# A hybrid attention block: the gates' stage in written order, decays in steps between its products, branch units in other places

## The chip, the cores and the metric

The kernel runs as one program on one core of a Trainium2 chip. The metric is the device time of one execution in microseconds. Before the change it is 2083.89 us, the median of 3 runs (2081.26 to 2083.93). On the core, TensorE multiplies matrices, VectorE and ScalarE do elementwise work, GpSimd helps with small things, and SyncE (SP) issues most of the DMA transfers, in the order of its queue.

## The reference

One layer of a streaming encoder works on 1024 frames and 16 meta tokens of width 1024, batch 1, all in float32:

```python
h = h + 0.5 * swiglu(rmsnorm(h, ffn1_norm), ...)
u = rmsnorm(h, mix_norm)
(aq, ak, av, gq, gk, gv, gr, g_low, gate_a, gate_b) = jnp.split(u @ w_in, offsets, axis=-1)
ya = window_sink_attention(aq, ak, av, att_sinks)         # 8 heads, 2 key heads, chunks of 64
z = g_low @ gla_gate_w + gla_gate_b
log_a = jax.nn.log_sigmoid(z) / 16
og = gated_linear_attention(gq, gk, gv, log_a)            # 4 heads, a recurrence over chunks
yb = rmsnorm(og, gla_out_norm) * jax.nn.silu(gr)
mixed = sigmoid(gate_a) * (ya @ w_branch_att) + sigmoid(gate_b) * (yb @ w_branch_gla)
h = h + mixed @ w_out
h = h + 0.5 * swiglu(rmsnorm(h, ffn2_norm), ...)
return rmsnorm(h, final_norm)[:, N_META:]
```

The change touches the two gates (`gate_a`, `gate_b`, 1024 columns each), the decays made from `log_a`, and the product `ya @ w_branch_att`.

## The kernel before

Activations lie with their features on the 128 partitions and tokens along the free axis. A float32 matrix product is done as three products of halves: `split` or `halves` cast a value to a high half on ScalarE (line 235 for activations and weights of this stage, line 132 for 1024-wide weights) and subtract it on VectorE to get the low half (lines 236 and 133). One pass of one 128 x 128 weight tile over 512 tokens is one matmul on TensorE.

The stages of the middle of the program, in order: plain projections (`together`, lines 915 to 928), the low-rank projection of the decay gate (`low_rank`, lines 941 to 950), the gates' stage, projections and window attention (from line 1114), the linear attention (`Gla`, from line 1433), and the branch of the linear attention with its gate (`ev_b`, line 1551).

**The gates' stage** computes 16 column groups of 128, for the two gates, in 8 pairs. A pair is a 2 x 2 block product with seven instead of eight block products (`PRODUCTS`, line 154, with sums of weight blocks S1 to S4 and of activations T1 to T4). Each product is 12 matmuls (line 460). `gate_pair` loads two weight tiles with DMA, `Group.sums` makes S1 to S4 on VectorE (line 443), `Group.weights` makes the two halves of a product's weights, and copies and additions take the sums out of PSUM into blocks called x, which go to the `gates` buffer in DRAM. Sigmoid isn't applied here, but where a gate is used: in `ev_a` (line 1371) for the attention branch and in `ev_b` for the other. After the pairs 2 to 12, `decay` (line 1051) does one of six pieces: for each of two head pairs two halves of 512 frames and the 16 meta tokens. A piece has one small matmul into the tile z (line 1056), then Abs, Exp and Ln on ScalarE, running sums on VectorE (line 1064), four more Exp, and products with the queries and keys, which go to DRAM. In this program the engines' order in this stage is set by the framework's scheduler.

T4 takes the place of an activation tile half (lines 1000 to 1004), saved in `b12_dram`; it is loaded back at the end of the stage (line 1106). Weight tiles come from a ring (`ring_tile`): six of the pool `w_main` and two of `w_more`. Blocks x, s and those of the decays come from one pool of 17.

**The branch units.** `branch_units` (line 1349) gives four units for 256 columns of the attention branch: two column groups for the first 512 tokens (chunk 0) and two for the last 512. A unit is 12 matmuls, a load of the gate, and `ev_a`. There are 16 units in the list `fill`: two are done in the attention's last two slots, four ahead of the linear attention, the rest between its steps (line 1525), the last one behind them. `out_gate` (line 1502) finishes a head of the linear attention with transposes into the tile ot. The recurrence runs over 8 steps for each of two head pairs (`products`, `step`).

Of the kernel before, what the change touches and what calls it, by code (L numbers as in the profile page):

```python
# [14 lines left out]
ALU = mybir.AluOpType  # L15
# [20 lines left out]
def hybrid_kernel(  # L36
# [968 lines left out]

    def gate_pair(m):

        pair = []
        for i in range(2):
            pair.append(raw_tile())  # L1010
            c = C_GA + (m + i) * P
            nc.sync.dma_start(out=pair[-1].rearrange("p (k m) -> p k m", k=KT),
                              in_=w_in[:, c:c + P].rearrange("(k p) m -> p k m", p=P))
        g = Group(g8, *pair)
        cols = [k * P for k in range(4)]

        def product(i):
            return g.product(i, g.weights(i), g8.tops, cols, 0, m)

        def keep(i, c, x):  # L1020
            nc.sync.dma_start(out=gates[m + i, :, c * 512:(c + 1) * 512], in_=x)

        b = product(0)
        x11, x22 = g8.block("x11"), g8.block("x22")
        nc.scalar.copy(x11, b)
        a = product(1)
        nc.vector.tensor_add(x11, a, x11)
        g.sums(nc.vector)
        keep(0, 0, x11)
        product(2)  # L1030
        x12 = g8.block("x12")
        nc.scalar.copy(x12, b)
        d = product(3)
        nc.scalar.copy(x22, d)
        product(4)
        nc.vector.tensor_add(x22, b, x22)
        keep(1, 1, x22)
        product(5)
        nc.vector.tensor_add(x12, d, x12)
        keep(0, 1, x12)  # L1040
        product(6)
        x21 = g8.block("x21")
        nc.scalar.copy(x21, b)
        keep(1, 0, x21)

# [5 lines left out]
    def decay(p, c0, n):  # L1051
# [5 lines left out]
        nc.scalar.activation(e, ps, AF.Abs, bias=bg)  # L1057
        nc.vector.tensor_scalar(b, ps, bg, 0.0, op0=ALU.add, op1=ALU.min)

        nc.scalar.activation(e, e, AF.Exp, scale=-1.0)  # L1060
        nc.scalar.activation(e, e, AF.Ln, bias=1.0)
        w = min(n, P)
        for a in range(0, n, w):
            nc.vector.tensor_tensor_scan(b[:, a:a + w], b[:, a:a + w], e[:, a:a + w], 0.0, op0=ALU.add, op1=ALU.subtract)
        if n == NM:
            nc.vector.tensor_scalar(e, b, -1.0, b[:, n - 1:n], op0=ALU.mult, op1=ALU.add)
            nc.scalar.activation(e, e, AF.Exp, scale=1.0 / 16.0)
            nc.vector.tensor_mul(e, k, e)
            nc.sync.dma_start(out=km_dram[p], in_=e)
            return  # L1070
        q, d = g8.block("q"), g8.block("d")
        nc.sync.dma_start(out=q, in_=gq_dram[p, :, c0:c0 + n])
        by = lambda t: t.rearrange("p (a b) -> p a b", b=P)
        at = lambda i: by(b)[:, :, i:i + 1].to_broadcast([P, n // P, P])

        def out(x, src):
            nc.sync.dma_start(out=scaled_dram[x][p, :, c0:c0 + n], in_=src)


        nc.scalar.activation(e, b, AF.Exp, scale=1.0 / 16.0)  # L1080
        nc.vector.tensor_copy(dec[p][:, c0 // P:(c0 + n) // P, :], by(e)[:, :, P - 1:P])
        nc.vector.tensor_mul(e, q, e)
        out("qi", e)
        nc.vector.tensor_tensor(by(d), at(P - 1), by(b), op=ALU.subtract)
        nc.scalar.activation(d, d, AF.Exp, scale=1.0 / 16.0)
        nc.vector.tensor_mul(d, k, d)
        out("kd", d)
        e = g8.block("e")
        nc.vector.tensor_tensor(by(e), by(b), at(63), op=ALU.subtract)
        nc.scalar.activation(b, e, AF.Exp, scale=1.0 / 16.0)  # L1090
        nc.vector.tensor_mul(q, q, b)
        out("qm", q)
        nc.scalar.activation(e, e, AF.Exp, scale=-1.0 / 16.0)
        nc.vector.tensor_mul(k, k, e)
        out("km", k)

    pieces = [(p, c0, n) for p in range(2) for c0, n in CH_FR + [(S, NM)]]
    for m in range(0, 16, 2):
        if m == 14:
            g8.ring = [w_main] * 6  # L1100
        gate_pair(m)
        if 2 <= m <= 12:
            decay(*pieces.pop(0))
    for k in range(4):
# [265 lines left out]
    def ev_a(ps, m, c0, n, g):  # L1370
        nc.scalar.activation(g, g, AF.Sigmoid)
        nc.vector.tensor_mul(g, ps[:, 0:n], g)
        nc.sync.dma_start(out=gates[m, :, c0:c0 + n], in_=g)
# [3 lines left out]
    for m0 in range(0, KT, 2):  # L1377
        views = [(slice(g * 64, g * 64 + 64), lambda r: r.rearrange("p (k m) -> p k m", k=4),
                  w_branch_att[g * 256:(g + 1) * 256, m0 * P:(m0 + 2) * P].rearrange("(i d) m -> d i m", d=64)) for g in range(2)]
        fill += branch_units(views, ya, m0, load_a, ev_a)  # L1380

# [137 lines left out]
    for p in range(2):  # L1519
        g = heads[p]  # L1520
        g.begin()
        g.products(0)
        g.state()
        for j in range(8):
            if j % 4 != 3 and len(fill) > 1:
                fill.pop(0)()
            if p == 1 and j in (1, 3, 5, 7):
                out_gate(j // 4, CH_FR[(j // 2) % 2:(j // 2) % 2 + 1])
            if j < 7:
                g.products(j + 1)  # L1530
            g.step(j)
        g.end()
# [233 lines left out]
```

## Time and profile before

| | |
|---|---|
| median of 3 runs | 2083.89 us |
| the profiled execution | 2084.47 us |
| its span, first to last instruction | 2082.8 us |
| TensorE matmul busy | 2014.3 us, 97% |
| VectorE busy | 1401.3 us, 67% |
| ScalarE busy | 890.3 us, 43% |
| mean granted TensorE clock | 0.985 |

The shares are averages over stages. TensorE's matmuls are pipelined, so a busy TensorE can still run at the lower of its two clock levels; the granted clock is a column of its own. Idle time of an engine counts where TensorE waits for it. In a timeline, the number in brackets is how long the engine had stood idle before the row, and what it waited for.

### The profile page before, as it was taken

To read this page: it belongs to the slowest core of one execution; us is meant where nothing else is said; L and a number is where in the kernel's file an instruction comes from. 1 tells how busy PE (TensorE), PEld (TensorE's weight loads), DVE (VectorE), ACT (ScalarE), POOL (GpSimd) and SP (SyncE) were. 2 spreads that over 40 slices of the span, in tenths; PEclk is the share of its full clock that TensorE was granted. 3 is DMA by queue.
4 is the path that set the end of the run, shared out by engine and by line. 5 is a ranking of instruction groups with operands and counts; after the bars stand their busy time and mean duration, and the time that the engine had idled before them with its cause. 6 is when DMAs were issued, how large, how long until landed. Compare 5 with 4: busy or idle time off the path is not lost.

```text
span 2082.8 us, 32065 instructions
## 1 busy us (share of the span) xinstructions
PE 2014.3 (97%) x12084; PEld 1782.2 (86%) x12084; DVE 1401.3 (67%) x2441; ACT 890.3 (43%) x1727; POOL 177.9 (9%) x205
## 2 busy tenths in 40 slices
PE   8899999999999999788999999999999999999998
PEld 8899999999999987566889867888888888878888
DVE  5866676676778784544357647757876776767885
ACT  5534444443322353444356645434444444442222
POOL 1000000001222000000500000020000000013212
PEclk9999999999999999899999999999999999999999
DMA  6333354349985342433412364752453453599822
GB/s 202 106 113 123 128 177 146 118 160 362 348 288 171 106 130 76 131 122 112 116 49 62 116 217 136 246 170 81 133 192 130 142 182 122 174 373 360 289 96 82
DMA packets 285772, 343.06 MB, mean 165 GB/s; under 512 B 26406, under 2 KB 192032, under 8 KB 285616
## 3 DMA queue, kind: packets, MB, share of 16 engines
q1 hardware_dynamic: 267968, 279.60, 40.5%
q10 hardware_dynamic: 17296, 61.29, 7.8%
q8 instruction: 95, 1.56, 0.3%
q14 instruction: 61, 0.50, 0.1%
q0 software_dynamic: 352, 0.11, 0.1%
HBM read 220.66 MB, written 120.27 MB: 164 GB/s over the span
## 4 chain that ended last, share of the span: by engine, by line
PE 89%; DMA 3%; ACT 3%; DVE 3%; issue 1%; SPq 0%; DVEq 0%; ACTq 0%; POOLq 0%
PE pb L460 30%; PE pd L460 16%; PE pa L460 9%; PE z L460 3%; PE pj L103 2%; PE pj L104 2%; PE pj L105 2%; PE br L103 1%; PE wo L103 1%; PE wo L105 1%; PE wo L104 1%; PE br L104 1%; PE br L105 1%; DMA f1mid<-kh 1%; PE pd L841 1%
## 5 line engine op out<-in xcount | busy, mean ns | idle before, releaser
L460 PE MATMUL pb<-tt,wop 128*128 128x260 f32 (+1 forms) x2040 | 343.5, 322 | 0.0
L460 PEld LDWEIGHTS pb<-tt,wop 128*128 128x128 f32 x2040 | 299.3, 188 | 29.0
L235 ACT CAST wop<-s 128x512 fp32r<-128x512 f32 x264 | 162.1, 621 | 241.2 <-PE pb L460 95.7
L236 DVE TENSOR_TENSOR wop<-s,wop 128x512 fp32r<-128x512 f32 x264 | 184.7, 708 | 89.2 <-ACT wop L235 88.6
L460 PE MATMUL pb<-tm,wop 128*128 128x260 f32 (+1 forms) x1440 | 235.9, 320 | 5.8 <-DVE h L347 3.5
L460 PEld LDWEIGHTS pb<-tm,wop 128*128 128x128 f32 x1440 | 208.6, 190 | 25.5 <-DVE h L347 4.0
L235 ACT CAST wop<-raw 128x512 fp32r<-128x512 f32 x198 | 122.4, 623 | 235.3 <-PE pb L460 105.2
L236 DVE TENSOR_TENSOR wop<-raw,wop 128x512 fp32r<-128x512 f32 x198 | 139.5, 710 | 28.3 <-ACT wop L235 27.8
L443 POOL TENSOR_TENSOR s<-raw 128x512 f32<-128x512 f32 x28 | 37.1, 1324 | 1057.2 <-DMA tm<-f1mid 454.8
L460 PE MATMUL pd<-tt,wop 128*128 128x260 f32 (+1 forms) x708 | 121.2, 324 | 0.1
L347 DVE SCALAR_TENSOR_TENSOR h<-pb,h 128x520 f32<-128x520 f32 (+1 forms) x136 | 93.9, 693 | 39.7 <-PE pb L460 37.6
L460 PE MATMUL pd<-tm,wop 128*128 128x260 f32 (+1 forms) x720 | 118.8, 319 | 0.0
L460 PEld LDWEIGHTS pd<-tt,wop 128*128 128x128 f32 x708 | 104.6, 188 | 11.2 <-DVE wop L236 0.6
L460 PE MATMUL pb<-tb,wop 128*128 128x260 f32 (+1 forms) x672 | 112.3, 320 | 0.5 <-ACT vec L94 0.5
L460 PEld LDWEIGHTS pd<-tm,wop 128*128 128x128 f32 x720 | 104.3, 188 | 9.4
L460 PE MATMUL pd<-tb,wop 128*128 128x260 f32 (+1 forms) x672 | 112.2, 320 | 0.0
L460 PE MATMUL pa<-tb,wop 128*128 128x260 f32 (+1 forms) x672 | 112.0, 320 | 0.0
L460 PEld LDWEIGHTS pb<-tb,wop 128*128 128x128 f32 x672 | 97.9, 188 | 10.0 <-ACT vec L94 0.6
L460 PEld LDWEIGHTS pd<-tb,wop 128*128 128x128 f32 x672 | 97.8, 188 | 9.4
L460 PEld LDWEIGHTS pa<-tb,wop 128*128 128x128 f32 x672 | 97.8, 188 | 9.4
L443 DVE TENSOR_TENSOR s<-raw 128x512 f32<-128x512 f32 x94 | 64.6, 688 | 56.6 <-DMA raw<-in_ffn_w_up 54.9
L347 DVE SCALAR_TENSOR_TENSOR h<-pd,h 128x520 f32<-128x520 f32 (+3 forms) x112 | 72.6, 654 | 33.7 <-PE pd L460 17.5
(446 smaller groups left out, 4163.8 us busy)
## 6 DMA issues: line engine op xcount, KB each, us to landing
tm<-f1mid ACTq DMA_DIRECT2D x56, 520.0 KB, 6.4
tm<-f2mid ACTq DMA_DIRECT2D x56, 512.0 KB, 6.2
raw<-in_ffn_w_gate SPq DMA_DIRECT2D x42, 512.0 KB, 3.9
raw<-in_ffn_w_up SPq DMA_DIRECT2D x42, 512.0 KB, 4.1
raw<-in_ffn_w_down SPq DMA_DIRECT2D x80, 256.0 KB, 5.4
f1mid<-kh SPq DMA_DIRECT2D x70, 260.0 KB, 3.1
f1mid<-kl SPq DMA_DIRECT2D x70, 260.0 KB, 3.0
f2mid<-kh SPq DMA_DIRECT2D x70, 256.0 KB, 2.8
```

Source lines behind the costliest of these rows:

```text
L103: nc.tensor.matmul(ps, wh[k], xh[k], start=(k == 0), stop=False)
L104: nc.tensor.matmul(ps, wh[k], xl[k], start=False, stop=False)
L105: nc.tensor.matmul(ps, wl[k], xh[k], start=False, stop=(k == n - 1))
L235: nc.scalar.copy(x[:, 0:n], src)
L236: nc.vector.tensor_sub(x[:, n:2 * n], src, x[:, 0:n].bitcast(F32))
L347: nc.vector.scalar_tensor_tensor(hm, ps, 0.5, hm, op0=ALU.mult, op1=ALU.add)
L443: (eng.tensor_add if add else eng.tensor_sub)(a[s], a[x], a[y])
L460: nc.tensor.matmul(ps, y, z[:, s0:s0 + sn], start=(first and k == 0 and at == 0), stop=(at == 2 and k == len(cols) - 1), skip_group_check= ...
L841: nc.tensor.matmul(ps, y, x[:, c0 + s0:c0 + s0 + sn], start=(n == 0), stop=(n == 3 * LAST - 1), skip_group_check=True)
```

## The change

The gates' stage is written as one loop over pairs and products, and ScalarE, VectorE and TensorE take its instructions in the order in which the code is written (`manual_schedule`). The weights of a product are split two products ahead, over the pair's end too; the next pair's sums are made in the last step of a pair. The next pair's weight tiles are loaded a pair earlier, into two pools in turn, and the ring has only the six tiles of `w_main`. `decay` is now a generator: it stops at each `yield`, and one step of it follows each product. The decays lie in the last four pairs, with two pieces in the second and fourth of them. The eight column groups of the attention gate get Sigmoid in this stage, in place (line 1018 of the changed kernel), so `ev_a` has none. The units of the branch come in another sequence (the first four all for chunk 0), fewer of them stand between the steps of the recurrence, and four stand behind it.

```diff
-    def gate_pair(m):
+    def gate_weights(m):
         pair = []
         for i in range(2):
-            pair.append(raw_tile())
+            pair.append(g8.ext_tile() if m % 4 else raw_tile())
...
+        return Group(g8, *pair)
+
+    def gate_out(m, i, c, x):
+        if m < KT:
+            nc.scalar.activation(x, x, AF.Sigmoid)
+        nc.sync.dma_start(out=gates[m + i, :, c * 512:(c + 1) * 512], in_=x)
+
+    def gate_evac(m, i, ps, xs):
+        if i in (0, 2, 3, 6):
+            x = xs[i] = g8.block("x")
+            nc.scalar.copy(x, ps)
+            if i == 6:
+                gate_out(m, 1, 0, x)
+        else:
+            x = xs[{1: 0, 4: 3, 5: 2}[i]]
+            nc.vector.tensor_add(x, ps, x)
+            gate_out(m, *{1: (0, 0), 4: (1, 1), 5: (0, 1)}[i], x)
...
         nc.scalar.activation(e, ps, AF.Abs, bias=bg)
         nc.vector.tensor_scalar(b, ps, bg, 0.0, op0=ALU.add, op1=ALU.min)
+        yield
         nc.scalar.activation(e, e, AF.Exp, scale=-1.0)
+        yield
         nc.scalar.activation(e, e, AF.Ln, bias=1.0)
+        yield
...
+        nc.vector.tensor_tensor(by(d), at(P - 1), by(b), op=ALU.subtract)
+        nc.vector.tensor_tensor(by(f), by(b), at(63), op=ALU.subtract)
+        yield
...
         nc.scalar.activation(e, b, AF.Exp, scale=1.0 / 16.0)
+        nc.scalar.activation(d, d, AF.Exp, scale=1.0 / 16.0)
         nc.vector.tensor_copy(dec[p][:, c0 // P:(c0 + n) // P, :], by(e)[:, :, P - 1:P])
+        yield
         nc.vector.tensor_mul(e, q, e)
         out("qi", e)
...
+    AHEAD, cols = 2, [k * P for k in range(4)]
+    g8.ring = [w_main] * 6
+    group, follow = gate_weights(0), gate_weights(2)
+    made = [group.weights(i) for i in range(AHEAD)]
+    group.sums(nc.vector)
+    manual = tc.manual_schedule(engines={nc.scalar.engine, nc.vector.engine, nc.tensor.engine})
+    manual.__enter__()
     for m in range(0, 16, 2):
-        if m == 14:
-            g8.ring = [w_main] * 6
-        gate_pair(m)
-        if 2 <= m <= 12:
-            decay(*pieces.pop(0))
+        others = [decay(*x) for x in pieces.pop(0)] if m >= KT else []
+        xs = {}
+        for i in range(7):
+            j = i + AHEAD
+            if j < 7:
+                made.append(group.weights(j))
+            elif follow:
+                made.append(follow.weights(j - 7))
+                if j == 8:
+                    follow.sums(nc.vector)
+            gate_evac(m, i, group.product(i, made.pop(0), g8.tops, cols, 0, m), xs)
+            for o in others:
+                next(o, None)
+        group, follow = follow, gate_weights(m + 4) if m + 4 < 16 else None
+    manual.__exit__(None, None, None)
...
     def ev_a(ps, m, c0, n, g):
-        nc.scalar.activation(g, g, AF.Sigmoid)
         nc.vector.tensor_mul(g, ps[:, 0:n], g)
...
-        fill += branch_units(views, ya, m0, load_a, ev_a)
+        fill.append(branch_units(views, ya, m0, load_a, ev_a))
+    fill = fill[0][0:2] + fill[1][0:2] + fill[0][2:4] + fill[1][2:4] + fill[2] + fill[3]
...
-            if j % 4 != 3 and len(fill) > 1:
+            if j % 2 == 0 and len(fill) > 4:
                 fill.pop(0)()
```

ScalarE before, from a pair's last copy (line 1043) over a decay piece to the next pair's casts; wop is a weight tile, s a sum of weights, raw a loaded weight tile, x an output block, and z, pa, pb, pd are PSUM tiles:

```order
L1043 COPY x_9760<-z 128x512
L1057 ACTIVATE e<-z,vec 128x512
L1060 ACTIVATE e<-e 128x512
L1061 ACT_TABLE_LOAD
L1061 ACTIVATE e<-e 128x512
L1080 ACT_TABLE_LOAD
L1080 ACTIVATE e<-b 128x512
L1085 ACTIVATE d<-d 128x512
L1090 ACTIVATE b<-e 128x512
L1025 COPY x_9815<-z 128x512
L1093 ACTIVATE e<-e 128x512
L235 CAST wop<-s 128x512 x4
```

The whole piece stands between the last copy of one pair and the casts of the next pair, four of which follow each other.

ScalarE now, in a pair with two decay pieces, from the copy behind product 2 to the cast in step 5; lines 1050, 1075, 1076 and 1058 belong to the decay, and raw_9902 is the loaded tile from which product 6's weights are cut:

```order
L1025 COPY x<-pb 128x512
L1050 ACT_TABLE_LOAD
L1050 ACTIVATE e<-e 128x512
L1050 ACTIVATE e<-e 128x16
L235 CAST wop<-s 128x512
L1025 COPY x<-pd 128x512
L235 CAST wop<-raw_9902 128x512
L1075 ACT_TABLE_LOAD
L1075 ACTIVATE e<-b 128x512
L1076 ACTIVATE d<-d 128x512
L1058 ACTIVATE e<-e 128x16
L235 CAST wop<-raw 128x512
```

Casts, copies and the steps of the decay alternate. Two table loads stand in this stretch, with a cast, a copy and a cast between their steps.

VectorE now, in the same pair, from the subtraction behind the cast of step 2 to that of product 6's weights (line 1054 is the running sum, 1068 and 1069 the two differences):

```order
L236 TENSOR_TENSOR wop<-s,wop 128x512 x2
L1054 SCALAR_TENSOR_TENSOR b<-b,e 128x128 x4
L1068 TENSOR_TENSOR d<-b 128x512
L1069 TENSOR_TENSOR f<-b 128x512
L1054 SCALAR_TENSOR_TENSOR b<-b,e 128x16
L1056 TENSOR_SCALAR e<-b 128x16
L236 TENSOR_TENSOR wop<-raw_9902,wop 128x512
```

The scans, differences and the small piece stand ahead of the subtraction that finishes product 6's weights. Before, all seven subtractions of a pair stood in a row:

```order
L443 TENSOR_TENSOR s<-raw 128x512
L443 TENSOR_TENSOR s<-s,raw 128x512
L443 TENSOR_TENSOR s<-raw 128x512
L443 TENSOR_TENSOR s<-raw,s 128x512
L236 TENSOR_TENSOR wop<-s,wop 128x512 x4
L236 TENSOR_TENSOR wop<-raw,wop 128x512 x3
L1036 TENSOR_TENSOR x_9816<-z,x_9816 128x512
L1039 TENSOR_TENSOR x_9859<-pa,x_9859 128x512
```

There the sums follow the whole decay piece, and the subtractions follow the sums.

SP's queue before, at the end of the stage: uh and ul are the halves loaded back from `b12_dram`, the transfers of line 124 with 8x64 load weights of the attention's queries:

```order
L124 DMA raw<-in_w_in 128x8x128 x2
L124 DMA raw<-in_w_in 128x8x64 x2
L1021 DMA gates<-x_10444 128x512
L124 DMA raw<-in_w_in 128x8x64
L1021 DMA gates<-x_10487 128x512
L1106 DMA uh_8384<-b_dram 128x512
L1106 DMA ul_8392<-b_dram 128x512
L1106 DMA uh_8385<-b_dram 128x512
```

Two halves of query weights and a third stand ahead of the first reload.

The same place now, from the last stores on (line 1117 is the reload, 1073 and 1061 are stores of the last decay, 1019 is a store of the gates); one half of the first query weights and one reload stand some rows ahead of these:

```order
L1061 DMA km_dram<-e 128x16
L1019 DMA gates<-x 128x512
L1073 DMA qm_dram<-q 128x512
L1073 DMA km_dram<-k 128x512
L1117 DMA ul_8392<-b_dram 128x512
L1117 DMA uh_8385<-b_dram 128x512
L1117 DMA ul_8393<-b_dram 128x512
L1117 DMA uh_8386<-b_dram 128x512
L1117 DMA ul_8394<-b_dram 128x512
L1117 DMA uh_8387<-b_dram 128x512
L1117 DMA ul_8395<-b_dram 128x512
L124 DMA raw<-in_w_in 128x8x64 x7
```

Seven reloads stand behind the last stores, and the other half of the first query weights follows the reloads, at the head of the seven transfers in the last row.

## Rows read from the trace of the kernel before

**Rows 1.** Windows: us, then PE, PEld, DVE, ACT, POOL busy, PEclk, DMA, GB/s.

```profile
789.20:996.06 206.86, 174.29 (x728) 135.91 (x726) 102.49 (x176) 91.27 (x149) 5.67 (x18) 0.92 0.38 117
...
789.20:794.89 5.69, 5.69 (x34) 3.40 (x32) 0.69 (x1) 1.71 (x4) 0.00 (x0) 1.00 0.12 46
...
796.68:798.70 2.02, 2.02 (x16) 1.77 (x17) 1.02 (x2) 1.67 (x4) 0.00 (x0) 1.00 0.00 0
...
851.19:873.20 22.01, 22.01 (x85) 17.26 (x85) 8.59 (x16) 8.31 (x14) 0.00 (x0) 0.88 0.37 107
...
1283.00:1289.00 6.00, 3.84 (x21) 3.17 (x19) 5.84 (x8) 4.08 (x6) 0.00 (x0) 0.78 0.24 87
```

**Rows 2.** Waits of TensorE, 789 to 997 us: us in total, times, longest.

```profile
PE z L460 <- ACT wop L235: 17.2, 4, 8.4
...
PE pa L460 <- ACT wop L235: 13.1, 2, 6.6
...
PE pj L103 <- ACT x L1043: 0.7, 1, 0.7
```

**Rows 3.** Chain of waits in the gates' stage: start us, us, what.

```profile
840.22 1.28 ACT L1061
...
841.51 0.64 ACT e L1061
...
842.18 1.38 DVE b L1064 x4
...
851.19 5.55 PE z L460 x12
...
859.50 2.72 PE z L460 x12
```

**Rows 4.** Timeline of TensorE around a decay matmul: start us, us, instruction, idle before.

```profile
800.70 0.49 PE L1056 MATMUL z<-glow,gw 96*128 96x512 f32 x1 [0.67 <-DVE glow L950]
...
801.03 0.39 PE L460 MATMUL pb<-uh,wop 128*128 128x512 f32 x1
```

**Rows 5.** Groups of ScalarE, 800 to 1000 us: busy us, mean ns, idle before.

```profile
L235 ACT CAST wop<-s 128x512 fp32r<-128x512 f32 x32 | 18.2, 618 | 14.0 <-DVE s L443 13.5
...
L1034 ACT COPY x<-pa 128x512 f32<-128x512 f32 x7 | 4.1, 588 | 7.5 <-PE pa L460 7.5
```

**Rows 6.** Groups of VectorE, 800 to 1000 us.

```profile
L236 DVE TENSOR_TENSOR wop<-s,wop 128x512 fp32r<-128x512 f32 x32 | 20.1, 685 | 3.4 <-ACT wop L235 3.4
...
L1027 DVE TENSOR_TENSOR x<-pa,x 128x512 f32<-128x512 f32 x7 | 4.8, 685 | 1.2 <-PE pa L460 0.9 <-ACT x L1025 0.3
```

**Rows 7.** DMA issues, 740 to 1000 us: KB each, median us to landing.

```profile
gates<-x SPq DMA_DIRECT2D x32, 256.0 KB, 2.0
...
raw<-in_w_in SPq DMA_DIRECT2D x5, 256.0 KB, 4.7
```

**Rows 8.** Timeline of SP's queue: one reload.

```profile
997.35 0.45 SPq L1106 DMA_DIRECT2D ul<-b_dram  x1
```

**Rows 9.** Timeline at the end of attention.

```profile
1196.29 0.17 DVE L1284 TENSOR_SCALAR mx<-mx 128x4 f32<-128x4 f32 x1
...
1198.32 0.47 ACT L1286 ACTIVATE p<-p,mx 128x210 f32<-128x210 f32 x1
...
1200.87 1.79 PE L1304 MATMUL tp<-ident,p 128*82 128x128 f32 x8 [4.51 <-DVE p L1289]
...
1208.46 0.96 PE L103 MATMUL br<-qs,whi 128*128 128x512 f32 x3 [1.22 <-ACT qs L1326]
```

**Rows 10.** Timeline of TensorE at the end of the linear attention.

```profile
1284.69 0.66 PE L1512 MATMUL ot<-ident,o 128*128 128x128 f32 x4 [0.99 <-DVE o L1500]
...
1286.52 2.79 PE L1512 MATMUL ot<-ident,o 128*128 128x128 f32 x12 [1.17 <-DVE o L1500]
```

**Rows 11.** Timeline of TensorE: first matmuls of two recurrence steps.

```profile
1233.98 0.49 PE L1470 MATMUL at<-gqm,gkm 64*128 64x128 f32 x4
...
1235.83 0.49 PE L1470 MATMUL at<-gqm,gkm 64*128 64x128 f32 x4
```

More of the change, by code (lines that the diff above doesn't have):

```diff
@@ L1013, in gate_pair @@
                               in_=w_in[:, c:c + P].rearrange("(k p) m -> p k m", p=P))
[L1014 to L1044, printed above, removed]
+        return Group(g8, *pair)
[13 more added lines that the diff above has]
+            gate_out(m, *{1: (0, 0), 4: (1, 1), 5: (0, 1)}[i], x)
     dec = [sml.tile([P, 8, 1], F32, tag="dec", name=f"dec{p}", bufs=2) for p in range(2)]
@@ L1070, in decay @@
             return
-        q, d = g8.block("q"), g8.block("d")
+        q, d, f = [g8.block(x) for x in ("q", "d", "f")]
         nc.sync.dma_start(out=q, in_=gq_dram[p, :, c0:c0 + n])
@@ L1074, in decay @@
         at = lambda i: by(b)[:, :, i:i + 1].to_broadcast([P, n // P, P])
+        nc.vector.tensor_tensor(by(d), at(P - 1), by(b), op=ALU.subtract)
+        nc.vector.tensor_tensor(by(f), by(b), at(63), op=ALU.subtract)
+        yield
         def out(x, src):
@@ L1080, in decay @@
         nc.scalar.activation(e, b, AF.Exp, scale=1.0 / 16.0)
+        nc.scalar.activation(d, d, AF.Exp, scale=1.0 / 16.0)
         nc.vector.tensor_copy(dec[p][:, c0 // P:(c0 + n) // P, :], by(e)[:, :, P - 1:P])
+        yield
         nc.vector.tensor_mul(e, q, e)
         out("qi", e)
-        nc.vector.tensor_tensor(by(d), at(P - 1), by(b), op=ALU.subtract)
-        nc.scalar.activation(d, d, AF.Exp, scale=1.0 / 16.0)
         nc.vector.tensor_mul(d, k, d)
         out("kd", d)
-        e = g8.block("e")
-        nc.vector.tensor_tensor(by(e), by(b), at(63), op=ALU.subtract)
-        nc.scalar.activation(b, e, AF.Exp, scale=1.0 / 16.0)
+        nc.scalar.activation(b, f, AF.Exp, scale=1.0 / 16.0)
+        nc.scalar.activation(f, f, AF.Exp, scale=-1.0 / 16.0)
+        yield
         nc.vector.tensor_mul(q, q, b)
         out("qm", q)
-        nc.scalar.activation(e, e, AF.Exp, scale=-1.0 / 16.0)
-        nc.vector.tensor_mul(k, k, e)
+        nc.vector.tensor_mul(k, k, f)
         out("km", k)
-    pieces = [(p, c0, n) for p in range(2) for c0, n in CH_FR + [(S, NM)]]
-    for m in range(0, 16, 2):
-        if m == 14:
-            g8.ring = [w_main] * 6
-        gate_pair(m)
-        if 2 <= m <= 12:
-            decay(*pieces.pop(0))
+    pieces = [[(p, *CH_FR[0])] if c == 0 else [(p, *CH_FR[1]), (p, S, NM)] for p in range(2) for c in range(2)]
+    AHEAD, cols = 2, [k * P for k in range(4)]
[5 more added lines that the diff above has]
+    manual.__enter__()
+    for m in range(0, 16, 2):
+        others = [decay(*x) for x in pieces.pop(0)] if m >= KT else []
[13 more added lines that the diff above has]
+    manual.__exit__(None, None, None)
     for k in range(4):
```

## The prediction

> **What bounds the kernel now.** I read the busy rows of the page first: TensorE works nearly the whole span, so only a stretch in which it stands still, or runs at the lower clock, can give time back. The windows then show where that is. From the first low-rank matmul to the first attention projection, 206.86 us, TensorE is busy for 174.29 and its mean granted clock is 0.92 of full speed [rows 1]: that is the gates' stage. The waits of TensorE there are 17.2 + 13.1 us on casts of weight halves, plus 0.7 at its end [rows 2]. The chain of waits tells why a cast is late: after each pair of gate columns one decay piece runs as a block, and its table loads, Ln, scans and products on ScalarE and VectorE stand ahead of the next pair's sums and casts, until TensorE starts again at 851.19 [rows 3]. The first product after such a wait takes 5.55 us, a product in the run 2.72 [rows 3]; in the 22 us behind it the granted clock is 0.88 [rows 1], which mixes the two levels 1.2 and 2.4 GHz.
>
> **What the stage must hold.** All its TensorE work is unchanged: low-rank matmuls 5.69 + 2.02 us [rows 1]; 8 pairs of 7 products, 56 x 2.72 = 152.3 [rows 3]; six decay matmuls of at most 0.33 (800.70 to 801.03 [rows 4]), 2.0; the last evacuation before the next stage, 0.7 [rows 2]. Sum 162.7. The stage takes 206.86, so 44.1 us are waits and slow clock, and that is what continuous feeding can return.
>
> **Does the new order feed it?** Weights are split two products ahead. In the written order the cast for product i+3 comes after the evacuation of product i, so the chain behind product i's end has two products, 5.44 us, and three for the cast after. In the first four pairs a step is an evacuation 0.59, a cast 0.62 [rows 5], a Sigmoid of about the same size (an estimate from these), and on VectorE a subtraction and an addition of 0.69 each [rows 6]: 3.2 us at most, one behind the other. No wait is left there.
>
> The four pairs with decays are tighter; two of them carry a 16-column piece besides the 512-column one. Counting whole such a pair: ScalarE 7 casts 4.3, 4 copies 2.4, 7 functions of about 0.64 = 4.5, 2 table loads 2.6, 4 small ones under 1.2: 15.0 of 19.4 us. VectorE 7 subtractions, 4 sums, 3 additions, 4 products, 2 differences and a min at 0.69 to 0.75 = 14.5, scans 1.4, small ones about 1.2: 17.1 of 19.4. Neither engine is the bound, but the order inside matters. The longest chain starts at the end of product 2: copy 0.59, table load 1.28, Ln 0.64 [rows 3], small Ln about 0.2, cast 0.62, subtraction 0.69, scans 1.38 [rows 3], two differences 1.38, small ones 0.4, and then the subtraction of product 6's weights 0.69: 7.9 us against three products, 8.16. It holds by 0.3 us; without the small piece by 0.9. Durations overlap a little between instructions, each semaphore takes a little back. So I bound the waits left: 0 from below; from above 2 us in each of four pairs, 8 us, which is two thirds of one VectorE instruction late in each link. I take 1.0, near the lower end, because the sum by rows closes.
>
> Where a wait is that short, does the clock fall as well? Only if it does would a product cost up to 2.8 us more (5.55 against 2.72 [rows 3]); I leave that to the range.
>
> ScalarE's table loads are where a rule speaks against the change. By rows, a load starts 0.01 us after the function before it can be done, and Ln starts at 841.51, 1.29 after the load's start at 840.22 [rows 3]: 1.28 is all it costs. The Trainium skill ("ScalarE: Activation LUTs", What ACT_TABLE_LOAD costs) adds a drain of 1.38 us to each load, 2.66 in all. By that rule the chain above would be 9.3 us against 8.16 and TensorE would wait. The trace does not show the drain, so I go by the rows.
>
> **The seam behind the stage.** The last pair now has a decay, and on SP's queue the reloads of the overwritten activation halves, seven of eight, stand behind its last stores; the second half of the first query weights stands behind those. If the stage ends at T, the last store is issued at about T + 1.2 (copy, then two products on VectorE), the reloads take about 3.8 (seven issues of 0.45 [rows 8] and some gaps, an estimate), and 256 KB of weights land 4.7 later [rows 7]: T + 9.7. A 1024-wide cast of about 1.1 (an estimate, twice 0.62 less the fixed part) makes T + 10.8. Two projection units of 24 matmuls stand before its use, 0.7 + 2 x 5.44 = T + 11.6. Covered by 0.8; bounds 0 and 4 us (a transfer 2 us later, slow clock behind it). I take 0.5.
>
> **Branch units.** Sigmoid of the attention gates leaves the attention loop. There it stood before the last softmax: the maxima are done at 1196.46, the exponentials start at 1198.32, TensorE gets its transposes at 1200.87 after 4.51 us [rows 9]. Without Sigmoid and its two table loads they start 1.86 earlier; VectorE's product with the gate still waits for the same transfer, but the exponentials cover it. The next unit waited 1.22 for the second half of the attention output [rows 9]; in the new sequence it reads the first half. With about 0.7 of slow clock (eight transposes took 1.79 behind the wait, four 0.66 elsewhere [rows 9, 10]) that is 3.8 us; bounds 1.2 (the wait only moves to the late transfer) and 5.
>
> At the end of the linear attention TensorE waits 0.99 + 1.17 for the normalised outputs [rows 10], and the window there shows clock 0.78 over 6 us [rows 1], at most 1.3 us. Four units, 4 x 2.72 = 10.9 us, now stand there instead of one. They cover it; the loads of the output gate then come late on SP's queue, so I count 2.8 of 3.5. Against it, ten steps of the recurrence instead of seven run without a unit. Such a step takes 1.85 us (1233.98 to 1235.83 [rows 11]) and shows no wait; I take 0, bounds 0 and 0.7 each, 2 us.
>
> **Sum.** Gates' stage -44.1 + 1.0 + 0.5; attention's end -3.8; linear attention's end -2.8: -49.2. The profiled run took 2084.47 (span 2082.8 and 1.7 around it), 0.6 above the median 2083.89; 2084.5 - 49.2 = 2035.3, on the median's level 2034.7. With every bound good the gain is 44.1 + 5 + 3.5 = 52.6, 2031; with the ordinary bad ones (5 us of waits, 4 at the seam, nothing from the units) 2048 at the far end, though not all at once. The likeliest case's own range is 2030 to 2043.
>
> **Rivals.**
> *The decay pairs still wait.* VectorE's backlog runs over the pair's end: in the last step of a pair a subtraction, four sums and two products, 7 x 0.69 = 4.8 us [rows 6], stand in 2.72, so it goes into the next pair 2.1 late, and the weights of its product 2 stand behind. If no slack takes that up, four pairs pay 2.1 each, 8.4: 2043. If each wait also slows one product by 2.8 [rows 3], 11.2 more: 2054. For it: the margin of 0.3 us that I count elsewhere in the pair. Against it: the two products ahead, and 17.1 of 19.4 us. Chance 0.12, for 2043 to 2054. The drain of the Trainium skill's ScalarE page would act in the same pairs: by it the two larger are over by 1.1 and the smaller by 0.4, 3.0 us or 2038, and with the slow product behind each wait 2049.
> *The units' new places give nothing.* The late transfer, not Sigmoid, sets the softmax, and the bare steps cost what the end returns: 2035 + 6.6 = 2041, with the 2 us of bare steps 2043. For it: ScalarE had to wait for that transfer as well. Against it: the exponentials need neither. Chance 0.05.
> *Slower than before.* The stores hold the evacuations. Every evacuation writes one of 17 blocks, whose last store must have landed; on one queue with waiting weight loads, a store held up holds ScalarE, which in written order holds every cast behind it. To eat 44.1 + 6.6 us in 32 stores takes 1.6 us beyond the slack each, so it decides from about 4.3 us of hold-up per store (slack 2.7). Against it: a store lands in 2.0 us [rows 7], and with 8 blocks a pair a block comes back two pairs later; in the decay pairs 14 or 17 are taken, and it still comes back one pair, 19 us, later. Chance 0.03.
> *It does not do what it says.* The compiled order could keep a decay as one block; the rows in the section on the change show it in steps. Then 2084, chance 0.02.
>
> **Numbers.** Forecast 0.78, rivals 0.12, 0.05, 0.03, 0.02. The range 2029 to 2049 holds the forecast, half of the first rival and the second. A measurement of this kernel tells apart about 0.2%, 4 us: faster 0.95, the same 0.02, slower 0.03.
>
> **What would show it.** Right: a stage of about 164 us with granted clock 1.00 throughout; no TensorE wait on a cast over 1 us; ten table loads in the stage with 1.28 us each; exponentials of the last softmax right after their maxima; no wait of the transposes behind the recurrence. Wrong: waits at products 2 or 6 of the last four pairs with a slow product behind; a wait of the first query unit; a linear-attention stretch longer by more than the work that moved.

## The result and the profile after

The changed kernel takes 2057.84 us (median of 4 runs, 2056.32 to 2058.72) against 2083.64 for the kernel before in the same runs: ratio 0.9878, 95% interval 0.9861 to 0.9895. Forecast were 2034.7 and a range of 2029 to 2049. It is faster, by 25.8 us where 49.2 were forecast.

The two profiled executions, cut at four instructions that both kernels have (us; the forecast's terms put into the stretches where they fall):

| stretch | before | after | difference | forecast |
|---|---|---|---|---|
| start to the first low-rank matmul | 789.20 | 786.25 | -2.95 | 0 |
| gates' stage | 206.86 | 179.91 | -26.95 | -43.1 |
| first attention projection to the last softmax's transposes | 204.81 | 210.55 | +5.74 | -1.4 |
| to the wait in the second feed-forward's way down | 672.49 | 667.66 | -4.83 | -4.7 |
| to the end | 209.44 | 211.13 | +1.69 | 0 |
| span | 2082.8 | 2055.5 | -27.3 | -49.2 |

The first stretch has the same work in all kernels, and took between 785.1 and 790.2 us in the twelve profiles of this study: its 2.95 is no gain. The last stretch has the same work in all too, and took 209.3 to 211.2. Two rows are wrong, the gates' stage by 16.2 us and the one behind it by 7.1.

Windows of the changed kernel, columns as in [rows 1]: the stage, two products in it, the attention stretch, a piece of that one.

```profile
786.25:966.16 179.91, 167.91 (x727) 133.45 (x726) 96.64 (x166) 93.92 (x160) 4.38 (x12) 0.98 0.39 120
922.81:927.26 4.45, 4.45 (x13) 3.50 (x13) 0.55 (x1) 0.12 (x1) 0.00 (x0) 0.62 0.70 204
946.59:951.01 4.42, 4.42 (x13) 3.51 (x14) 0.93 (x2) 1.92 (x5) 0.00 (x0) 0.61 0.28 75
966.16:1176.71 210.55, 202.72 (x1200) 175.56 (x1200) 120.50 (x373) 110.28 (x311) 23.47 (x60) 0.98 0.31 92
981.67:987.60 5.93, 5.92 (x17) 4.96 (x18) 1.56 (x1) 0.00 (x0) 5.33 (x12) 0.50 0.43 91
```

TensorE is busy for 167.91 of the stage's 179.91 us; 12.0 us are still waits. Which, the waits of TensorE in that window tell (they answer to [rows 2]):

```profile
PE z L460 <- DVE b L1045: 4.1, 2, 2.4
PE z L1043 <- DVE b L1045: 2.5, 1, 2.5
PE pb L460 <- DVE x L1030: 1.6, 2, 0.8
PE pb L460 <- ACT x L1025: 1.4, 2, 0.7
PE pb L1043 <- ACT x L1025: 1.4, 2, 0.7
PE pj L103 <- DVE x L1030: 1.0, 1, 1.0
```

No cast of a weight half (L235) is left among them: the 30.3 us of [rows 2] are gone, and the weights do come in time. What TensorE waits for instead are readers of PSUM: the min of a decay (L1045), the copies (L1025) and the additions (L1030). The largest, as a timeline of all engines at the start of the pair m = 12:

```profile
920.01 0.40 PE L1043 MATMUL z<-glow,gw 96*128 96x512 f32 x1
920.21 0.68 DVE L1086 TENSOR_TENSOR q<-q,b 128x512 f32<-128x512 f32 x1
...
920.81 0.68 DVE L1088 TENSOR_TENSOR k<-k,f 128x512 f32<-128x512 f32 x1
...
921.41 0.68 DVE L236 TENSOR_TENSOR wop<-s,wop 128x512 fp32r<-128x512 f32 x1
...
922.01 0.74 DVE L1045 TENSOR_SCALAR b<-z,vec 128x512 f32<-128x512 f32 x1
...
922.81 0.73 PE L460 MATMUL z<-uh,wop 128*128 128x512 f32 x1 [2.40 <-DVE b L1045]
```

The decay's matmul fills z at 920.01. VectorE has two products of the previous decay and a subtraction ahead in its queue, and reads z at 922.01. The next product of the gates (product 1), whose weights are ready, starts only when that is over. Its output is also called z, though it is another accumulator: in this stage `bank` cuts PSUM tiles of 128 x 1024, two banks, into halves of 512 columns, and a tile has the name of its first half. The next product accumulates into the half beside the decay's.

Behind the stage, SP's queue, ScalarE and TensorE (rows of three timelines; the reloads have line 1117, `raw` is the query weight):

```profile
969.79 0.40 SPq L1073 DMA_DIRECT2D km_dram<-k  x1
970.24 0.45 SPq L1117 DMA_DIRECT2D ul<-b_dram  x1
...
973.34 0.42 SPq L1117 DMA_DIRECT2D ul<-b_dram  x1
973.81 10.44 SPq L124 DMA_DIRECT2D raw<-in_w_in  x5
...
980.58 1.05 ACT L132 CAST whi<-raw 128x1024 fp32r<-128x1024 f32 x1 [5.53 <-DMA raw<-in_w_in]
...
981.67 0.79 PE L103 MATMUL pj<-uh,whi 128*128 128x512 f32 x1 [4.37 <-ACT whi L132]
```

The order is the one that the forecast gave, the times are later: a wait of 4.37 us, and 5.93 us at clock 0.50 behind it.

At the two other places the waits went as forecast. TensorE at the last softmax (2.69 for 4.51 in [rows 9], and the unit behind it does not wait), and at the normalised outputs (one run of 16 transposes without a wait, for 0.99 and 1.17 in [rows 10]; a wait of 0.67 on the cast of the branch's input stands behind it, where the kernel before has none):

```profile
1176.71 1.13 PE L1315 MATMUL tp<-ident,p 128*82 128x128 f32 x8 [2.69 <-DVE p L1300]
1177.60 0.48 PE L103 MATMUL br<-qs,whi 128*128 128x512 f32 x1
...
1257.11 1.91 PE L1523 MATMUL ot<-ident,o 128*128 128x128 f32 x16
...
1261.53 0.50 PE L103 MATMUL br<-ybh,whi 128*128 128x512 f32 x1 [0.67 <-ACT ybh L108]
```

### The profile page after: what moved, and what is told of

Same layout as the page of the kernel before. It is cut to its first block, busy times and chain, and to the rows that moved or that the text cites. A ratio compares the mean times of both kernels' runs of the same rounds, so it can differ in the third digit from the quotient of the medians.

```text
span 2055.5 us, 32054 instructions
## 1 busy us (share of the span) xinstructions
PE 2006.4 (98%) x12084; PEld 1776.6 (86%) x12084; DVE 1403.1 (68%) x2441; ACT 882.2 (43%) x1722; POOL 178.4 (9%) x205
## 4 chain that ended last, share of the span: by engine, by line
PE 86%; DMA 5%; DVE 4%; ACT 3%; issue 1%; SPq 0%; DVEq 0%; ACTq 0%; POOLq 0%
PE pb L460 32%; PE pd L460 17%; PE pa L460 9%; PE pj L103 2%; PE pj L104 2%; PE pj L105 2%; PE wo L103 1%; PE wo L104 1%; PE wo L105 1%; PE br L103 1%; DMA raw<-in_ffn_w_down 1%; PE br L105 1%; PE br L104 1%; PE pd L841 1%; DMA f1mid<-kh 1%
## 5 line engine op out<-in xcount | busy, mean ns | idle before, releaser
L460 PE MATMUL pb<-tt,wop 128*128 128x260 f32 (+1 forms) x2112 | 361.1, 324 | 1.6 <-DVE x L1030 1.6
L460 PEld LDWEIGHTS pb<-tt,wop 128*128 128x128 f32 x2112 | 312.7, 188 | 34.2 <-DVE x L1030 2.4
L235 ACT CAST wop<-s 128x512 fp32r<-128x512 f32 x264 | 163.7, 621 | 236.7 <-PE pb L460 90.0
L235 ACT CAST wop<-raw 128x512 fp32r<-128x512 f32 x198 | 122.9, 621 | 220.5 <-PE pb L460 108.4
L460 PE MATMUL pd<-tt,wop 128*128 128x260 f32 (+1 forms) x816 | 146.4, 332 | 0.0
L460 PEld LDWEIGHTS pd<-tt,wop 128*128 128x128 f32 x816 | 124.9, 188 | 15.0
L103 PE MATMUL pj<-uh,whi 128*128 128x512 f32 (+2 forms) x256 | 93.1, 364 | 5.4 <-ACT whi L132 4.4
```

Of the source, the lines that this page charges most:

```text
L103: nc.tensor.matmul(ps, wh[k], xh[k], start=(k == 0), stop=False)
L235: nc.scalar.copy(x[:, 0:n], src)
L460: nc.tensor.matmul(ps, y, z[:, s0:s0 + sn], start=(first and k == 0 and at == 0), stop=(at == 2 and k == len(cols) - 1), skip_group_check= ...
```

## The experiments

Each was timed in runs of its own beside the kernel before, whose median was 2083.27 to 2084.24 in them. The experiments come from three chips; times are compared across them because the medians of the kernel before lie within 1.0 us.

**Single banks.** The pool of eight single banks, which the changed kernel opens behind the stage, is opened ahead of it:

```diff
+    dbl["open"] = False
+    doubles.close()
+    psp = ctx.enter_context(tc.tile_pool(name="psp", bufs=8, space=PSUM))
     AHEAD, cols = 2, [k * P for k in range(4)]
```

> The changed kernel with one edit: in the gates' stage every accumulator and every decay tile z gets a PSUM bank of its own (a pool of eight single banks, opened ahead of the stage) instead of half of a double tile of two banks. Theory A (shared double tile): in the changed kernel a matmul into one half waits until ScalarE or VectorE has read the other half. Those waits are 0.68 + 0.78 in two pairs, 0.68 twice before decay matmuls, 1.69, 2.40 and 2.45, together 10.8 us; behind the two longest a product takes 4.4 instead of 2.72, 3.5 us; and each restart costs about 0.17, 1.2 us. They all go: the stage takes 179.9 - 15.5 = 164.4 us, the kernel 2057.8 - 15.5 = 2042.3. Theory B (the engines are late anyway): the 6.5 us of the last three pairs come from VectorE's backlog behind the sums, and turn into waits on weight halves of the same size, with the slow products behind them; only the 0.7s go, about 5 us, 2053.

Measured: 2042.26 us, ratio 0.9803 (0.9789 to 0.9818). ScalarE and VectorE have the same instructions in the same order in the stage as in the changed kernel; only the tiles differ: eight halves of four tiles before, eight tiles now. The waits of TensorE in the stage and its window:

```profile
PE pb L460 <- DVE glow L950: 1.9, 1, 1.9
PE pj L945 <- DVE glow L950: 1.3, 1, 1.3
```

```profile
787.32:953.14 165.82, 162.39 (x728) 132.03 (x726) 95.01 (x164) 93.00 (x159) 3.31 (x11) 1.00 0.41 129
```

All the waits of the changed kernel's stage are gone, and none on a weight half came in their place: theory A. The time is that of its sum, though by other terms than it had: the stage takes 165.82 instead of 164.4. None of the six weight loads of the decay matmuls has a wait on a semaphore here; in the changed kernel three of them have one, two on ScalarE's (at 878.04 and 898.28) and one on VectorE's (at 946.46). So these waits stood in the program, put there by the way in which it tracks its tiles. The two new waits, 3.2 us, are the handover from the old pool to the new one, which has to wait for the last reader of the low-rank products.

**Reloads behind the first three units.** The loop of the reloads is moved in the code:

```diff
-    for k in range(4):
-        for i, x in enumerate(halves_of(k, 1)):
-            nc.sync.dma_start(out=x.bitcast(F32), in_=b12_dram[k, i])
...
     for units in firsts:
         units.pop(0)()
+    for k in range(4):
+        for i, x in enumerate(halves_of(k, 1)):
+            nc.sync.dma_start(out=x.bitcast(F32), in_=b12_dram[k, i])
```

> The changed kernel with one edit: the eight reloads of activation halves are written behind the first three projection units, so that both halves of the first query weights go ahead of them on SP's queue. Theory A (order on the queue): the second half was issued at 973.81, behind the last store (970.2) and seven reloads, and landed 6.7 us later; TensorE waited 4.37 us and its next 6 us ran at the lower clock. Issued with the first half at 964, it lands long before its use. The stretch from the first attention projection to the last softmax's transposes shrinks by 7.5 us, the kernel takes 2057.8 - 7.5 = 2050.3. Theory B (the transfers behind the stage are bound together): the reloads are then late instead, and the first unit on the second half of the tokens waits 2 to 4 us for them: 2053 to 2057.

Measured: 2051.46 us, ratio 0.9843 (0.9828 to 0.9858). SP's queue, and the window of the stretch to the last softmax:

```profile
966.62 1.01 SPq L124 DMA_DIRECT2D raw<-in_w_in  x2
...
973.04 0.39 SPq L1073 DMA_DIRECT2D km_dram<-k  x1
973.53 0.41 SPq L1227 DMA_DIRECT2D uh<-b_dram  x1
```

```profile
968.86:1171.85 202.99, 199.54 (x1200) 173.49 (x1200) 120.10 (x373) 110.15 (x311) 24.59 (x60) 1.00 0.32 95
```

Both halves now go ahead of the last stores, the reloads behind them, and no projection unit waits for either. The stretch is 7.56 us shorter, the median of the time 6.4. Theory A: the reloads are not late either, as theory B had it.

**Both.**

> Both edits in one kernel: single banks in the gates' stage, and the reloads behind the first three units. If the two losses are what separates the forecast of 2034.7 from the 2057.8 measured, their sum is -23 us: 2034.8, with a stage of 164.4 us and no wait of a projection unit. Rival: with the stage shorter the last pair's stores and the query weights come closer together, or VectorE's backlog shows as waits on weights; then 2040 to 2048.

Measured: 2035.8 us, ratio 0.9767 (0.9753 to 0.9782). The two losses add up, and with both gone the time is within 1.1 us of the forecast, in part by luck: in the profiled execution the stage is 3.7 us longer than the 163.7 of the forecast's sum, and the first stretch, with the same work, 3.9 shorter than before. The stage takes 167.44 us instead of the 164.4 expected: the same handover waits of 1.31 and 1.93 us, and here the 4.6 us behind them ran at a mean clock of 0.63:

```profile
796.60:801.20 4.60, 4.58 (x13) 3.64 (x14) 0.00 (x0) 0.03 (x1) 0.00 (x0) 0.63 0.00 0
```

**Both, with the pool opened ahead of the last plain projection.** The three lines stand in front of `together([(4, ch)])`.

> Both edits as before (single banks, reloads behind the first three units), with the eight single banks opened earlier, ahead of the last plain projection instead of behind the low-rank projection. There the handover of the PSUM pools cost 1.31 and 1.93 us of waits on the last reader of the old pool, and in the run with both edits a product at the lower clock. Theory A: ahead of the plain projection only one evacuation has to be waited for; the stage falls from 167.4 to 163.5 us and the kernel from 2035.8 to about 2032. Rival: the handover's wait only moves to its new place, 2035 to 2036.

Measured: 2032.45 us (2031.36 to 2034.32), ratio 0.9754 (0.974 to 0.9769), the fastest of all. No wait of TensorE over 0.1 us is left in the stage:

```profile
789.34:951.25 161.91, 161.76 (x727) 132.21 (x726) 95.08 (x164) 93.12 (x159) 3.30 (x11) 1.00 0.42 132
```

That is what the stage must hold: the forecast put it at 162.7.

**Decays whole behind a pair's last product**, on the kernel with both edits:

```diff
-            for o in others:
-                next(o, None)
+            if i == 6:
+                for o in others:
+                    for _ in o:
+                        pass
```

> Both edits (single banks, reloads behind the first three units), and the decays of a pair done whole behind its last product instead of a step behind each product; the written order and the weights two products ahead stay. Theory A (the steps are needed): a piece is a chain of about 9.9 us on ScalarE and VectorE, one with the small piece about 14; the two products whose weights are ready cover 5.4, so the third product of the next pair waits 5.8, 10.3 and 5.8 us, with a slow product of 2.8 more behind each: 2035.8 + 30 = 2066. Theory B (two products ahead do most of it): waits of 2 to 3 us, 2040 to 2046.

Measured: 2063.64 us, ratio 0.9901 (0.9887 to 0.9916): 27.8 more. TensorE's three waits, the first with the two rows of ScalarE ahead of it (the cast of product 2's weights and the copy of product 0):

```profile
902.21 0.60 ACT L235 CAST wop<-s 128x512 fp32r<-128x512 f32 x1
...
902.72 0.58 ACT L1025 COPY x<-pb 128x512 f32<-128x512 f32 x1
...
903.34 5.27 PE L460 MATMUL pb<-tt,wop 128*128 128x512 f32 x12 [5.54 <-ACT x L1025]
...
932.98 5.49 PE L460 MATMUL pb<-tt,wop 128*128 128x512 f32 x12 [7.62 <-ACT x L1025]
...
959.64 4.49 PE L460 MATMUL pb<-tt,wop 128*128 128x512 f32 x12 [4.25 <-ACT x L1025]
```

Theory A, with the middle wait 2.7 us and the last 1.6 us shorter than worked out. Two things hold product 2, both on ScalarE behind the decay: the cast of its own weights, which theory A had, and the copy of product 0, which neither theory had. Product 2 adds to the accumulator of product 0 and must wait until that is copied out. The copy ends last, 0.5 us behind the cast at each of the three waits, so the run doesn't separate the two: with either of them early, the other would still have held product 2 to within 0.5 us. The steps free both.

**One product ahead**, on the kernel with both edits: `AHEAD` is 1, and the next pair's sums stay in the last step (`j == 7`).

> Both edits, and weights split one product ahead instead of two (the next pair's sums still in the last step of a pair). Theory A: the chain behind a product has 5.4 us for what takes 7.9 in the larger decay pairs, and at each pair's end four sums stand ahead of the subtraction for the next product; waits of about 2.4 us in four pairs with slow products, and up to 2.1 at seven pair ends: 2035.8 + 26 = 2062. Theory B: one product ahead is enough, since neither engine is over 90% busy: 2036 to 2040.

Measured: 2047.21 us, ratio 0.9821 (0.9807 to 0.9836): 11.4 more, between the theories. There are nine waits of 0.41 to 0.85 us, 5.2 in all, one to three in each decay pair, such as these (and two of 0.2), and the stage takes 177.41 for 167.44:

```profile
908.72 3.29 PE L460 MATMUL pb<-tt,wop 128*128 128x512 f32 x12 [0.51 <-ACT wop L235]
913.02 0.74 PE L460 MATMUL pd<-uh,wop 128*128 128x512 f32 x2 [0.56 <-DVE wop L236]
```

None is as long as theory A had it, and the pairs without decays show none: in them one product ahead is enough, in the decay pairs it isn't. Why the stage loses 10 us with 5.2 of waits I did not follow further than that the products behind them are longer too.

**The scheduler's order**, on the kernel with both edits: `manual_schedule` is left out.

> Both edits, with the order of ScalarE, VectorE and TensorE in the gates' stage left to the framework's scheduler; the code itself (steps, two products ahead, Sigmoid in place) is the same. Theory A (the written order matters): the scheduler puts casts early and the evacuations or decay steps late, or again a decay as one run of instructions; waits of 6 to 8 us come back in the decay pairs: 2050 to 2070. Theory B (the structure of the code is enough): 2036 to 2040.

Measured: 2039.98 us, ratio 0.9787 (0.9771 to 0.9803). The stage takes 168.73, 1.3 more than in the written order; two waits of 0.28 are new, and one long one, at the fifth product of the first decay pair, which adds to an accumulator that a copy still has to read:

```profile
889.51 3.01 PE L460 MATMUL pb<-tt,wop 128*128 128x512 f32 x12 [1.61 <-ACT x L1025]
```

Theory B: steps, two products ahead, and pieces spread over the last four pairs do nearly all of it. The medians differ by 4.2 us with overlapping intervals, and the trace shows 1.3 of it in the stage.

**Units in their old places**, on the changed kernel: `fill` in its old sequence, and the old condition `j % 4 != 3 and len(fill) > 1`.

> The changed kernel with the branch units in their old sequence and old places (seven bare recurrence steps, one unit behind the last), Sigmoid still in the gates' stage. The forecast counted the new places at 2.8 us at the end of the linear attention, and 1.2 plus about 0.7 us at the end of attention, where the unit waited for the second half. Theory A: these waits come back, 2057.8 + 4.7 = 2062.5, with waits of about 1.0 + 1.2 us on the normalised outputs behind the recurrence and about 1.2 us in front of the first unit. Theory B: the places are worth nothing, since ten bare steps cost what the ends give: 2057.8.

Measured: 2063.56 us, ratio 0.9904 (0.9888 to 0.9921): 5.7 more. The waits of [rows 9] and [rows 10] are back, 1.21 for 1.22, 0.98 for 0.99, and 1.17:

```profile
1186.62 0.98 PE L103 MATMUL br<-qs,whi 128*128 128x512 f32 x3 [1.21 <-ACT qs L1337]
...
1263.12 0.66 PE L1522 MATMUL ot<-ident,o 128*128 128x128 f32 x4 [0.98 <-DVE o L1510]
1264.95 2.46 PE L1522 MATMUL ot<-ident,o 128*128 128x128 f32 x12 [1.17 <-DVE o L1510]
```

Theory A.

**Sigmoid back in `ev_a`**, on the fastest kernel.

> The kernel with single banks opened ahead of the last plain projection and the reloads behind the first three units (2032.45), with Sigmoid of the attention gates back in the evacuation of the attention branch; the units' new places stay. The forecast counted 1.9 us for it at the end of attention, where Sigmoid and two table loads stood ahead of the last exponentials. Theory A: with the units in their new places the transposes of the last softmax wait 4.5 instead of 2.7 us again, nothing else changes: 2034.3. Theory B (the scheduler now finds another place for it): no change, 2032.4.

Measured: 2036.68 us, ratio 0.9774 (0.9758 to 0.979), whose interval overlaps that of the fastest kernel. The trace decides: the wait at the last softmax is 4.04 instead of 2.68, and ScalarE has the load, Sigmoid and the second load ahead of the exponentials again:

```profile
1151.89 1.24 PE L1313 MATMUL tp<-ident,p 128*82 128x128 f32 x8 [4.04 <-DVE p L1298]
```

```profile
1145.14 1.28 ACT L1380 ACT_TABLE_LOAD   x1
1147.39 0.63 ACT L1380 ACTIVATE ga<-ga 128x512 f32<-128x512 f32 x1 [0.97 <-DMA ga<-gates]
1148.04 1.28 ACT L1295 ACT_TABLE_LOAD   x1
1149.33 0.47 ACT L1295 ACTIVATE p<-p,mx 128x210 f32<-128x210 f32 x1
```

1.4 us there, for 1.9 expected, and 2.3 behind it (671.45 for 669.17 in the stretch to the second feed-forward), which theory A did not have, and which I did not follow further. The two profiled executions take the same time, 2034.36 and 2034.32, since the first stretch, with the same work, was 3.7 us shorter here. What Sigmoid costs in that place depends on when its gate arrives: ScalarE waited 0.97 us for it here, 1.45 in the kernel before and 2.84 in the next experiment, and TensorE then 4.04, 4.51 and 5.89; without Sigmoid it waits 2.68 or 2.69 in every kernel. The stage itself is the same, 161.93 for 161.91: eight column groups of Sigmoid cost nothing in it.

**The kernel before with single banks**: the three lines in front of `together([(4, ch)])` in the kernel before.

> The kernel before, with one edit: the eight single PSUM banks opened ahead of the last plain projection, so that no two tiles of the gates' stage share a double one. Theory A: there the scheduler's order kept the sharing from showing, the waits stood on casts behind the decay pieces; 2084 unchanged, within 2 us. Theory B: the sharing already cost the kernel before some of its waits, as the changed one, and the time falls by 5 to 15 us, 2069 to 2079.

Measured: 2080.15 us, ratio 0.9988 (0.9979 to 0.9997): 3.1 us less, between the theories and nearer to A. Long waits on the casts stay, such as these two:

```profile
850.06 5.51 PE L460 MATMUL pb<-tt,wop 128*128 128x512 f32 x12 [8.42 <-ACT wop L235]
...
956.18 5.37 PE L460 MATMUL pb<-tt,wop 128*128 128x512 f32 x12 [6.91 <-ACT wop L235]
```

So the sharing cost the kernel before about 3 us. In the changed kernel the single banks gave 15.6 with the handover's waits, and 19.0 where they are opened at this same place (2051.46 to 2032.45, both with the reloads moved).

## Why the prediction was wrong, step by step

**What the stage must hold: right.** 162.7 us were counted, and the stage without waits takes 161.91.

**Whether the order feeds it: right for the weights, and this is the step that failed.** The forecast took continuous feeding of weights for all that TensorE needs ("that is what continuous feeding can return") and counted the six decay matmuls as 0.33 us of work each. It followed each instruction that a weight half waits for, and none that an accumulator waits for. In the trace no weight half is late. But z and the products' accumulators lie two to a tile, and a matmul into one half waits until the other half is read. With 12.0 us of waits in place of the 0.7 + 1.0 that were counted, 10.3 are missing in the sum; two products at clock 0.62 and 0.61 take 4.45 and 4.42 instead of 2.72, 3.4 more; the rest of the 16.2, 2.4, is spread over products that take some 0.1 to 0.3 longer behind the shorter waits. Single banks gave back 15.6 us in the time. The chain that was followed held: counted as 7.9 us, it took 7.6, from the end of product 2 at 906.06 to product 6's weights at 913.70.

**The backlog at a pair's end** was seen and sized: 2.1 us late. It stood among the rivals as a delay of the weights of product 2, where slack takes it up. What it really held was the min of the next decay, and through the shared tile TensorE: 1.69, 2.40 and 2.45 us, at three pairs instead of the four that were counted, since the first pair with a decay has none ahead of it. The rival's 8.4 to 19.6 us hold the 16.2 that the stage lost, and with the seam put right the time is 2051.46, inside its 2043 to 2054; but it had the wrong victim. So the signs that were named for it, waits at products 2 or 6, did not come: the waits of the decay pairs stand at product 1 and at the decay matmuls.

The kernel's code showed the sharing (`bank` and `double`, which cut one tile for two callers); in the rows of before it hardly shows, since the longer waits on casts stand in its place. The Trainium skill ("Perfetto Trace Analysis", Matmuls) says that independent matmul groups should rotate through different PSUM banks, so that the evacuation of one overlaps the matmuls of the next. These groups do lie in different banks, and the overlap was lost all the same until each had a tile of its own; the runs show that the tile counts, not the bank alone. The waits are semaphores of the program, not something that the chip added: the weight load at 946.46 carries one on VectorE, and with single banks no weight load of a decay carries any.

**The seam: the mechanism was right, its size wrong.** Forecast were 0.5 us. TensorE's last product ended at 966.16 - 1.01 = 965.15, T. The last store was to be issued at T + 1.2 and was at 969.79, T + 4.6: behind the last copies VectorE had an addition and five products of the last decays, not two. From there to the issue of the weights it took 4.0 us, with 3.8 counted for the reloads. The weights landed 6.7 us after their issue instead of 4.7, at T + 15.4 for T + 9.7, and were cast at T + 16.5, against a cover to T + 12.2. The 4.7 of [rows 7] was a median of loads in two places, and the trace of before tells them apart, three issued ahead of the reloads and two right behind them:

```profile
raw<-in_w_in SPq DMA_DIRECT2D x3, 256.0 KB, 3.3
...
raw<-in_w_in SPq DMA_DIRECT2D x2, 256.0 KB, 5.9
```

The load of the forecast is one of the second kind, so 1.2 of the 2.0 us could have been read there. The wait of 4.37 and half of 5.93 at clock 0.50 make 7.3, and the reloads behind the units gave 7.56 back in the stretch. The stated bound of 4 us was too narrow as well: it held the transfer's delay, but not the later stores with it.

**ScalarE's table loads: right.** A copy ends at 906.85 in the changed kernel, the load starts at 906.87 and its function at 908.16:

```profile
906.26 0.59 ACT L1025 COPY x<-pb 128x512 f32<-128x512 f32 x1 [4.93 <-PE pb L460]
906.87 1.28 ACT L1050 ACT_TABLE_LOAD   x1
908.16 0.73 ACT L1050 ACTIVATE e<-e 128x512 f32<-128x512 f32 x2
```

Nothing but the load's 1.28 stands between. The drain of the Trainium skill ("ScalarE: Activation LUTs", What ACT_TABLE_LOAD costs) shows here no more than before, and the longest chain, for which it would have given waits on weights, has none, nor has it in the fastest kernel, where no other wait lends it time.

**Branch units: right.** -6.6 us were forecast. The wait at the softmax fell by 1.82 (1.86), the stretch behind it by 4.83 (4.7), the waits came back with the old places, and ten bare steps cost nothing that shows. That 1.82 comes so close is in part luck of the trace: the same wait, which ends with a transfer, was 5.89 in the kernel before with single banks.

**Slower, or no effect:** no evacuation waits for a store, and the order is the one written.

**The range** of 2029 to 2049 missed by the stage: its waits on accumulators, 12.0 us where 0.7 were counted, had no bound at all. With single banks alone the time is 2042.26, inside the range, though the seam's loss is still there; with the seam alone put right it is 2051.46, outside. The seam's 7.3 us lay beyond its own bound of 4.

## What to carry to other kernels

When TensorE is to be fed without a gap, list for each matmul both sides: what it reads, and who must have read the PSUM tile that it writes, with the queue that this reader stands in. Two callers that share a tile share each other's readers, even if they never touch the same bank; a small side matmul whose reader stands in a full queue is the worst neighbour for an accumulator. At the end of a stage, count every instruction between the last product and the last store before saying what a queue behind it can start.

## What the runs showed of the hardware that I had not expected

- The same two waits, 1.31 and 1.93 us with 2.2 us of matmuls between them, stand in five kernels. Over the 4.6 us behind them the granted clock was 1.00 in three (single banks alone, decays whole, the scheduler's order) and 0.63 in two (both edits, one product ahead). Behind the waits of 2.40 and 2.45 in the changed kernel products took 4.45 and 4.42 us, at 0.62 and 0.61 of full clock. A slow product behind a wait of some 2 us is a risk to put into a range, not a term to count on.
- Loads of 256 KB of weights in pieces of 64 columns landed 2.9 to 4.5 us after their issue where they stood ahead of the reloads, and 5.6 to 7.3 where they stood right behind seven or eight of them, in five kernels (before, changed, single banks, reloads moved, both edits).
